# Update of the decoding states of a gated DeltaNet: full-array matmuls on masked keys, or pairs of 32-row strips on plain keys

## The chip, the cores and the metric

The kernel runs on one core of one Trainium2 chip. The metric is the time of one execution on the device in microseconds, the median of several runs. The engines are PE (TensorE, with its weight loads PEld), DVE (VectorE), ACT (ScalarE), POOL (GpSimd) and SP (SyncE, which issues most of the transfers).

## The reference

The program is one inference step of a hybrid decoder layer: a normed and modulated input of 256 prompt tokens and 8 x 4 decoding tokens goes through one large projection, three token mixers (a gated MLP over chunks, a gated DeltaNet, sparse attention) and one output projection. The change lies in the DeltaNet, in the part for the decoding tokens. For each of 16 heads and each of 8 decoding sequences there is a state S of 128 x 128 (key by value). In one chunk of 4 tokens:

```python
G = jnp.cumsum(gc, axis=-1)
...
kg = kc * jnp.exp(G[..., -1:] - G)[..., None]
gl = jnp.exp(G[..., -1])

def step(s, xs):
    qg_i, kg_i, u_i, w_i, attn_i, gl_i = xs
    v_new = u_i - jnp.einsum('bhcd,bhde->bhce', w_i, s)
    o = jnp.einsum('bhcd,bhde->bhce', qg_i, s) + jnp.einsum('bhcs,bhse->bhce', attn_i, v_new)
    s = s * gl_i[..., None, None] + jnp.einsum('bhcd,bhce->bhde', kg_i, v_new)
    return s, o
```

The last line of the step, `s = ...`, is what the changed code computes. It is an outer product over 4 tokens only, for 128 pairs of head and sequence.

## The kernel before, in words

The large projections are run as many matmuls with a moving operand of 288 columns (256 prompt and 32 decoding tokens) and weights of 128 x 128, named acc. Weights and activations are split in two parts of a shorter mantissa (wh, wl and hH, hL), so that one tile takes three matmuls: acc<-hH,wh, acc<-hL,wh and acc<-hH,wl. ACT makes wh from the loaded w (a cast), DVE makes wl (a subtraction). These matmuls form a stream that runs through the whole program.

Everything else (convolutions, DeltaNet, attention, gating) is written as small generators, called chains here, that yield where they wait for another engine. A planner, the class Weaver, runs when the program is built: it holds an estimated time for each engine and decides which chain takes its next step between two acc units. The order that results is fixed in the program; each engine runs its own list in that order. All instructions are recorded by one helper, so all rows of the profile carry its line, L71, and are told apart by the names of their tiles. Rules of the planner that matter here:

- `bank(n)` (L284) takes n of four PSUM banks for a chain and yields until they are free by the planner's estimate; `free()` gives one back.
- `calm()` (L273) holds a chain back until the planner's DMA estimate allows a transfer.
- `finish(gens)` (L245) steps the named chains, and others that can run, until they are done, without going on with the stream.
- `gmlp_open` (L2149) begins with `W.finish([DN[3]])`: the last DeltaNet group must be done before the buffers of the gating MLP are opened. It is called ahead of one fixed unit of the stream, `u[GMO].pre.append(gmlp_open)` (L2337, GMO = 12).

The DeltaNet is worked in four groups of four heads. dn_all (L1705) runs dn_group for the prompt tokens and then dn_sample (L1976) for the 32 decoding tokens of four heads, laid out as 128 rows: row 32 h + 4 b + t is head h, sequence b, token t. dn_sample loads a row of gates GB and the output gate z, clears a mask tile M, transposes q, k and v (sT), takes norms (ACT, then POOL: rr, sc), scales keys and values (kb, vb), makes kbT, the gram matrices, UA and A, and then the products with the states in blocks of 16 small matmuls on column strips (kS and qS, state_mm, L2036), between them U, Ys, vs and osm. M lies in the buffer R4, from which the prompt part of the same group writes its last output (mixD) to memory.

Then update() (L2089) is pushed as a chain of its own, beside the rest of dn_sample (the norm of the output, oTs, the write of mixD). It makes eight copies of the new values, vk[:, b], each zero outside the rows of sequence b. For the keys a tile kgm had been made, `kgm[q, hl]` = the scaled keys in the 32 rows of head hl, and zero in the other 96. For each head and each half of the sequences one matmul over all 128 rows, kgm[:, hl] by four of the vk side by side (128 x 512), gives the four outer products in one bank, named Sup; four DVE instructions (scalar_tensor_tensor) then make S * exp(g_last) + product. After a head the state is written to memory.

Of the kernel before, what the change touches and what calls it, by code (L numbers as in the profile page):

```python
# [14 lines left out]
OP = mybir.AluOpType  # L15
# [4 lines left out]
P = 128  # L20
# [67 lines left out]
class Weaver:  # L88
# [195 lines left out]
    def bank(self, n=1):  # L284

        yield
        while not self.room(n):
            yield lambda: self.room(n)
        self.take(n)
# [8 lines left out]
    def free(self, n=1):  # L298
        self.banks -= n
        self.bank_free += [self.end] * n  # L300
# [74 lines left out]
def tile_hybrid_step(ctx: ExitStack, tc: tile.TileContext, I, O):  # L375
    nc = tc.nc
    W = Weaver()
    V, A, G, T, S = (Eng(W, k, e) for k, e in zip("VAGTS", (nc.vector, nc.scalar, nc.gpsimd, nc.tensor, nc.sync)))
    dma, dma2 = S.dma_start, S.dma_start
    bank, free = W.bank, W.free  # L380
# [17 lines left out]
    def tl(pool, shape, name, bufs=1, dt=F32, tag=None):  # L398
        return W.tile(pools[pool][1], shape, dt, tag or name, name, bufs)

    def pr(name="pr"):
        t = psum.tile([P, 512], F32, tag="r", name=name, bufs=N_BANK)
        W.bank_use[t.tensor.name] = ("T", 0.0)
        return t

    def pr4(name="pr"):
        return pr(name).rearrange("p (c n) -> p c n", c=4)
# [491 lines left out]
    at_, n = [0], la_end[0] + LEAD0  # L899
# [3 lines left out]
    i = 0  # L903
    while i < len(lb):
# [4 lines left out]
        for j, u in enumerate(us):  # L909
            e = min(len(la), n0 + int(rate * (j + 1)) // PAIR * PAIR)  # L910
            W.units += [u] + la[n:e]
            n = e
        i = nxt
# [777 lines left out]
    def place(name, n):  # L1691

        t = tl("dn", [P, n * P], name, 1)

        def cut(o, *shape):
            v = t[:, o * P:(o + math.prod(shape[:-1])) * P] if len(shape) > 1 else t[:, o * P:(o + 1) * P]
            names = "abc"[:len(shape) - 1]
            if len(shape) > 1:
                v = v.rearrange(f"p ({' '.join(names)} n) -> p {' '.join(names)} n",
                                **dict(zip(names, shape[:-1])), n=shape[-1])  # L1700
            return v

        return cut

    def dn_all(g, convs):  # L1705
        yield lambda: all(c.done for c in convs) and (g - 1 in MAIN if g else X.g_smp.done)
        if g == 0:
            close_pool("ap")
            open_pool("dn")
        b = Box()  # L1710
        yield from dn_group(g, b)
        yield from dn_sample(g, b)
        if g == 3:
            close_pool("dn")
# [261 lines left out]
    def dn_sample(g, b):  # L1976
        q0 = 32 + g
        St, b_ld = b.St, b.ld
        ya, yb, ye, yf = (place(f"R{r}", 8) for r in (0, 1, 4, 5))
        GB, df, kb, vb, kbT, Pm, Y, vn0 = (ya(i, P) for i in range(8))  # L1980
        UA, AM, dec = (yb(i, 2, P) for i in (0, 2, 4))
        M = ye(0, 8, P).rearrange("p a (c n) -> p (a c n)", n=32).rearrange("p (h b n) -> p h b n", h=4, b=NB)
        kgm, vn1, os_, junk = yf(0, 4, P), yf(4, P), yf(5, P), yf(7, P)
        z = yf(6, P).rearrange("p (h t) -> p h t", h=4)
        dma2(GB, GrD[q0:q0 + 1].to_broadcast([P, P]))
        dma2(z, zD[2 + g][:, :, NPR:NTOK])
# [5 lines left out]
        pa = pr4("sT")  # L1992
# [11 lines left out]
        sc = tl("dn", [P, 6], "sc", 4)  # L2004
# [2 lines left out]
        G.tensor_tensor(sc[:, 4:5], sc[:, 0:1], eG[:, q0:q0 + 1], op=OP.mult)  # L2007
        G.tensor_scalar(sc[:, 4:5], sc[:, 4:5], -1.0, None, op0=OP.mult)
        V.tensor_scalar(df, GB, Gc[:, q0:q0 + 1], 0.0, op0=OP.subtract, op1=OP.min)
        G.memset(kgm, 0.0)  # L2010
        yield
        A.activation(kb, pa[:, 1], AF.Copy, scale=sc[:, 0:1])
        A.activation(vb, pa[:, 2], AF.Copy, scale=hbeta[:, q0:q0 + 1])
        for hl in range(4):
            q = slice(32 * hl, 32 * hl + 32)
            V.tensor_scalar(kgm[q, hl], pa[q, 1], sc[q, 2:3], None, op0=OP.mult)
        free()
        gl = tl("dn", [P, 32], "gls", 1)
        A.activation(gl, GB.rearrange("p (a t) -> p a t", t=NS)[:, :, NS - 1], AF.Exp)
# [69 lines left out]
        def update():  # L2089
            vk = place("R4", 8)(0, NB, P)  # L2090
            for b in range(NB):
                V.tensor_scalar(vk[:, b], vn1, bsel[:, b:b + 1], None, op0=OP.mult)
            for hl in range(4):
                for b0 in (0, 4):
                    yield from bank()
                    pu = pr("Sup")
                    T.matmul(pu, kgm[:, hl], vk[:, b0:b0 + 4].rearrange("p c n -> p (c n)"), start=True, stop=True)
                    yield
                    for b in range(b0, b0 + 4):
                        i = 8 * hl + b  # L2100
                        V.scalar_tensor_tensor(St[hl][:, b], St[hl][:, b], gl[:, i:i + 1],
                                               pu[:, (b - b0) * P:(b - b0 + 1) * P], op0=OP.mult, op1=OP.add)
                    free()
                yield from W.calm()
                dma(O[10][0, :, 4 * g + hl].rearrange("b d e -> d b e"), St[hl])

        MAIN[g] = True
        (up,) = W.push(update())
        yield
        r = yield from out_norm([os_], rq[:, 0:1], 1, junk)  # L2110
# [232 lines left out]
    mixed, n = [], 0  # L2343
    for i, u in enumerate(ph2):
        e = min(len(gates), int((i + 1 - GATE0) / GATE)) // GPAIR * GPAIR
        mixed += [u] + gates[n:e]
        n = max(n, e)
# [117 lines left out]
```

## Time and profile before

| | |
|---|---|
| median of 3 runs | 2639.03 us (2635.15 to 2641.7) |
| the profiled execution | 2654.27 us |
| its span, first to last instruction | 2652.5 us |
| mean granted clock of TensorE | 0.986 |
| busy: PE, PEld | 2560.9 us (97%), 2279.1 us (86%) |
| busy: DVE, ACT, POOL | 1623.5 us (61%), 1062.0 us (40%), 492.3 us (19%) |
| matmul records of Sup | 64, from 1521.7 to 2165.4 us |

The profiled execution is one run with the profiler on; its time and the durations in its rows belong together, and it is somewhat longer than the median of the timed runs. A matmul's row gives its duration from start to end; since matmuls overlap, what one costs in the stream is read from the starts of its neighbours. Consecutive records of one kind are shown as one row with their number.

### The profile page before, as it was taken

The numbers are of one execution on the slowest core, as the hardware profiler recorded it, in microseconds if no ns is written. First come the engines' busy times: TensorE is split into PE (matmuls) and PEld (weight loads), VectorE is DVE, ScalarE is ACT, GpSimd is POOL, SyncE is SP. The second block draws the span as 40 slices with busy tenths as digits, with TensorE's granted clock in tenths as the row PEclk, the third lists the DMA queues.
The fourth block names the chain that finished last, engine by engine and source line by source line (L and its number), as shares of the span: only waits on it lengthen the run. The fifth ranks groups of instructions, "written<-read, shape, count | busy, mean of one in ns | idle before, by whom it ended". The sixth has DMA issues, their size and how long they took to land.

```text
span 2652.5 us, 55324 instructions
## 1 busy us (share of the span) xinstructions
PE 2560.9 (97%) x21190; PEld 2279.1 (86%) x21190; DVE 1623.5 (61%) x3611; ACT 1062.0 (40%) x2440; POOL 492.3 (19%) x1137
## 2 busy tenths in 40 slices
PE   6999999999999999999999999999999999999997
PEld 3788888888888888877789989989989989999997
DVE  3477665555568786744467576567566567555554
ACT  3423222222245343333344444444443544444443
POOL 2000000000001042153543333343340210000000
PEclk9999999999999999999999999999999999999998
DMA  8999998998757576686776676577568565555565
GB/s 289 345 320 321 342 315 296 304 312 307 232 153 217 178 238 217 200 283 221 266 233 192 182 242 207 177 241 233 179 195 261 149 202 181 178 182 175 177 186 164
DMA packets 376032, 616.11 MB, mean 232 GB/s; under 512 B 48840, under 2 KB 149436, under 8 KB 375768
## 3 DMA queue, kind: packets, MB, share of 16 engines
q1 hardware_dynamic: 364728, 574.66, 67.8%
q0 software_dynamic: 11040, 37.92, 4.3%
q8 instruction: 167, 2.74, 0.4%
q14 instruction: 97, 0.79, 0.1%
HBM read 587.54 MB, written 24.95 MB: 231 GB/s over the span
## 4 chain that ended last, share of the span: by engine, by line
PE 86%; DMA 6%; DVE 2%; issue 2%; POOL 2%; ACT 1%; SPq 0%; another core or an unknown queue 0%; ACTq 0%; POOLq 0%; DVEq 0%
PE acc L71 68%; PE ada L71 7%; DMA wa<-in_w_ada_dram 2%; PE kT L71 1%; PE Sup L71 1%; DMA kraw<-in_cache_k_dram,ixk 1%; DVE wl L71 1%; PE YP L71 1%; DMA w<-in_w_in_dram 1%; PE v L71 1%; PE gram L71 1%; DMA vraw<-in_cache_v_dram,ixv 1%; PE o L71 1%; POOL vraw L71 1%; PE S L71 0%
## 5 line engine op out<-in xcount | busy, mean ns | idle before, releaser
L71 DVE TENSOR_TENSOR wl<-w,wh 128x512 fp32r<-128x512 f32 (+1 forms) x1216 | 806.1, 682 | 735.3 <-ACT wh L71 667.8
L71 ACT CAST wh<-w 128x512 fp32r<-128x512 f32 (+1 forms) x1216 | 717.3, 611 | 1232.3 <-PE acc L71 905.6
L71 PE MATMUL acc<-hH,wh 128*128 128x288 f32 (+1 forms) x3744 | 1180.2, 315 | 14.5 <-ACT hH L71 7.4
L71 PE MATMUL acc<-hL,wh 128*128 128x288 f32 (+1 forms) x3744 | 1110.4, 297 | 0.6 <-DVE hL L71 0.4
L71 PE MATMUL acc<-hH,wl 128*128 128x288 f32 (+1 forms) x3744 | 1108.4, 296 | 2.6 <-DVE wl L71 1.8
L71 PEld LDWEIGHTS acc<-hH,wh 128*128 128x128 f32 (+1 forms) x3744 | 708.4, 189 | 152.0 <-issue 81.9
L71 PEld LDWEIGHTS acc<-hL,wh 128*128 128x128 f32 (+1 forms) x3744 | 710.1, 190 | 6.7 <-issue 5.5
L71 PEld LDWEIGHTS acc<-hH,wl 128*128 128x128 f32 (+1 forms) x3744 | 709.1, 189 | 4.0 <-DVE wl L71 3.6
L71 PE MATMUL acc<-mL,wh 128*128 128x288 f32 x1024 | 302.6, 295 | 2.6 <-DVE mL L71 2.6
L71 PE MATMUL acc<-mH,wh 128*128 128x288 f32 x1024 | 304.4, 297 | 0.0
L71 PE MATMUL acc<-mH,wl 128*128 128x288 f32 x1024 | 302.7, 296 | 0.0
L71 PEld LDWEIGHTS acc<-mL,wh 128*128 128x128 f32 x1024 | 193.0, 189 | 2.9 <-DVE mL L71 2.9
L71 PEld LDWEIGHTS acc<-mH,wh 128*128 128x128 f32 x1024 | 193.0, 188 | 0.2
L71 PEld LDWEIGHTS acc<-mH,wl 128*128 128x128 f32 x1024 | 193.0, 188 | 0.0
L71 PE MATMUL ada<-wa,cT 128*32 128x256 f32 x2048 | 159.2, 395 | 15.8 <-DMA wa<-in_w_ada_dram 14.3
L71 PEld LDWEIGHTS ada<-wa,cT 128*32 128x32 f32 x2048 | 50.2, 109 | 66.9 <-issue 39.8
L71 DVE TENSOR_TENSOR zb<-zb,acc 128x288 f32<-128x288 f32 x160 | 70.9, 452 | 47.0 <-PE acc L71 45.7
L71 POOL TENSOR_TENSOR htmp<-yT,gaT 128x32 f32<-128x32 f32 x20 | 7.7, 382 | 460.0 <-DVE gaT L71 460.0
L71 PE MATMUL ada<-w,cT 128*32 128x256 f32 x1024 | 83.9, 393 | 1.9 <-issue 1.0
L71 POOL TENSOR_SCALAR frs<-frs 128x1 f32<-128x1 f32 (+1 forms) x3 | 0.9, 298 | 451.5 <-DVE frs L71 451.3
L71 DVE TENSOR_TENSOR R<-R,R 128x248 f32<-128x248 f32 (+30 forms) x248 | 72.6, 293 | 7.1 <-DMA R<-dD 0.5
L71 POOL TENSOR_SCALAR tap<-xp,cwT 128x32 f32<-128x32 f32 x144 | 75.8, 527 | 0.3
(457 smaller groups left out, 2387.0 us busy)
## 6 DMA issues: line engine op xcount, KB each, us to landing
w<-in_w_in_dram SPq DMA_DIRECT2D x464, 512.0 KB
wa<-in_w_ada_dram SPq DMA_DIRECT2D x160, 512.0 KB
w<-in_w_ada_dram SPq DMA_DIRECT2D x128, 512.0 KB
w<-in_w_out_dram SPq DMA_DIRECT2D x128, 512.0 KB
wa<-in_w_ada_dram SPq DMA_DIRECT2D x192, 256.0 KB
St<-in_state_dn_dram SPq DMA_DIRECT2D x16, 512.0 KB
out_dram<-St SPq DMA_DIRECT2D x16, 512.0 KB
X<-in_x_prompt_dram SPq DMA_DIRECT2D x8, 512.0 KB
```

The lines of the kernel that those rows point to most:

```text
L71: r = f(*a, **k)
```

## The change

kgm becomes kg, a tile of 128 x 128 that holds the scaled keys of all four heads, made by one DVE instruction; the memset of kgm is gone. In update() two heads are treated together: two banks are taken, and two matmuls follow each other, each on the 32 rows of its head (`tile_position=(32 * hl, 0)`), each into its own bank. Then come eight DVE instructions. The loop over the halves of the sequences lies inside the pair of heads, and the two states are written behind both halves.

```diff
--- before.py
+++ after.py
@@ -1980,7 +1980,7 @@
         GB, df, kb, vb, kbT, Pm, Y, vn0 = (ya(i, P) for i in range(8))
         UA, AM, dec = (yb(i, 2, P) for i in (0, 2, 4))
         M = ye(0, 8, P).rearrange("p a (c n) -> p (a c n)", n=32).rearrange("p (h b n) -> p h b n", h=4, b=NB)
-        kgm, vn1, os_, junk = yf(0, 4, P), yf(4, P), yf(5, P), yf(7, P)
+        kg, vn1, os_, junk = yf(0, P), yf(4, P), yf(5, P), yf(7, P)
         z = yf(6, P).rearrange("p (h t) -> p h t", h=4)
         dma2(GB, GrD[q0:q0 + 1].to_broadcast([P, P]))
         dma2(z, zD[2 + g][:, :, NPR:NTOK])
@@ -2007,13 +2007,10 @@
         G.tensor_tensor(sc[:, 4:5], sc[:, 0:1], eG[:, q0:q0 + 1], op=OP.mult)
         G.tensor_scalar(sc[:, 4:5], sc[:, 4:5], -1.0, None, op0=OP.mult)
         V.tensor_scalar(df, GB, Gc[:, q0:q0 + 1], 0.0, op0=OP.subtract, op1=OP.min)
-        G.memset(kgm, 0.0)
         yield
         A.activation(kb, pa[:, 1], AF.Copy, scale=sc[:, 0:1])
         A.activation(vb, pa[:, 2], AF.Copy, scale=hbeta[:, q0:q0 + 1])
-        for hl in range(4):
-            q = slice(32 * hl, 32 * hl + 32)
-            V.tensor_scalar(kgm[q, hl], pa[q, 1], sc[q, 2:3], None, op0=OP.mult)
+        V.tensor_scalar(kg, pa[:, 1], sc[:, 2:3], None, op0=OP.mult)
         free()
         gl = tl("dn", [P, 32], "gls", 1)
         A.activation(gl, GB.rearrange("p (a t) -> p a t", t=NS)[:, :, NS - 1], AF.Exp)
@@ -2090,19 +2087,26 @@
             vk = place("R4", 8)(0, NB, P)
             for b in range(NB):
                 V.tensor_scalar(vk[:, b], vn1, bsel[:, b:b + 1], None, op0=OP.mult)
-            for hl in range(4):
+
+            for h0 in (0, 2):
                 for b0 in (0, 4):
-                    yield from bank()
-                    pu = pr("Sup")
-                    T.matmul(pu, kgm[:, hl], vk[:, b0:b0 + 4].rearrange("p c n -> p (c n)"), start=True, stop=True)
+                    yield from bank(2)
+                    pus = []
+                    for hl in (h0, h0 + 1):
+                        pus.append(pr("Sup"))
+                        q = slice(32 * hl, 32 * hl + 32)
+                        T.matmul(pus[-1], kg[q], vk[q, b0:b0 + 4].rearrange("p c n -> p (c n)"), start=True, stop=True,
+                                 tile_position=(32 * hl, 0))
                     yield
-                    for b in range(b0, b0 + 4):
-                        i = 8 * hl + b
-                        V.scalar_tensor_tensor(St[hl][:, b], St[hl][:, b], gl[:, i:i + 1],
-                                               pu[:, (b - b0) * P:(b - b0 + 1) * P], op0=OP.mult, op1=OP.add)
-                    free()
-                yield from W.calm()
-                dma(O[10][0, :, 4 * g + hl].rearrange("b d e -> d b e"), St[hl])
+                    for hl, pu in zip((h0, h0 + 1), pus):
+                        for b in range(b0, b0 + 4):
+                            i = 8 * hl + b
+                            V.scalar_tensor_tensor(St[hl][:, b], St[hl][:, b], gl[:, i:i + 1],
+                                                   pu[:, (b - b0) * P:(b - b0 + 1) * P], op0=OP.mult, op1=OP.add)
+                        free()
+                for hl in (h0, h0 + 1):
+                    yield from W.calm()
+                    dma(O[10][0, :, 4 * g + hl].rearrange("b d e -> d b e"), St[hl])
 
         MAIN[g] = True
         (up,) = W.push(update())
```

The order that the planner makes is another. The first place is PE at the start of dn_sample for the last group: sT are the transposes of q, k and v, kbT and gram come next in that chain, and acc is the stream. Before:

```order
L71 MATMUL acc_26067<-hH_7380,wh 128x288
L71 MATMUL acc_26067<-hL_7452,wh 128x288
L71 MATMUL acc_26067<-hH_7380,wl 128x288
L71 MATMUL sT<-ident,SSG 128x128 x3
L71 MATMUL acc_26011<-hH_7380,wh 128x288
L71 MATMUL acc_26011<-hL_7452,wh 128x288
L71 MATMUL acc_26011<-hH_7380,wl 128x288
```

After:

```order
L71 MATMUL acc_26850<-hL_5268,wh 128x288
L71 MATMUL acc_26850<-hH_5196,wl 128x288
L71 MATMUL sT<-ident,SSG 128x128 x3
L71 MATMUL kbT<-ident,R_27082 128x128
L71 MATMUL gram<-R_27082,SSG 128x128
L71 MATMUL gram<-SSG 128x128
L71 MATMUL A<-ident,R_27083 128x128
L71 MATMUL kS_27142<-St_25406,R_27084 32x128
```

Before, acc matmuls follow behind sT (48 of them up to kbT). After, the whole chain follows without one.

The second place is PE at the end of the same group's update; vTk belongs to the gating MLP that is opened next. Before:

```order
L71 MATMUL Sup<-R_27182,R_26721 128x512
L71 MATMUL acc_26959<-hH_5196,wh 128x288
L71 MATMUL acc_26959<-hL_5268,wh 128x288
L71 MATMUL acc_26959<-hH_5196,wl 128x288
L71 MATMUL Sup<-R_27182,R_26721 128x512 x5
L71 MATMUL acc_26924<-hH_6288,wh 128x288
L71 MATMUL acc_26924<-hL_6360,wh 128x288
L71 MATMUL acc_26924<-hH_6288,wl 128x288
L71 MATMUL vTk<-ident,uv 128x128 x2
L71 MATMUL vTk<-ident,uv 32x128
```

After:

```order
L71 MATMUL qS_27187<-St_25409,R_27084 32x128
L71 MATMUL osm<-R_27085,R_27083 128x128
L71 MATMUL oTs<-ident,R_27085 128x128
L71 MATMUL Sup<-R_27243,R_27085 128x512 x8
L71 MATMUL acc_26801<-hH_6288,wh 128x288
L71 MATMUL acc_26801<-hL_6360,wh 128x288
L71 MATMUL acc_26801<-hH_6288,wl 128x288
L71 MATMUL vTk<-ident,uv 128x128 x2
L71 MATMUL vTk<-ident,uv 32x128
```

Before, there are acc matmuls between the first Sup, and five follow each other at the end. After, all eight stand together behind oTs, with no acc between osm and the last of them.

The third place is DVE at the same end: the row with bsel makes the eight vk, the St rows are the updates of the states, wl is the stream's subtraction, and the R row with oTs is the end of the output's norm. Before:

```order
L71 TENSOR_TENSOR R_26721<-osm,R_26721 128x128
L71 TENSOR_TENSOR wl<-w,wh 128x512
L71 TENSOR_SCALAR R_27182<-R_26721,bsel 128x128 x8
L71 TENSOR_TENSOR wl<-w,wh 128x512 x2
L71 TENSOR_SCALAR R_26721<-R_26721,onr 128x128
L71 SCALAR_TENSOR_TENSOR St_25133<-St_25133,gls,Sup 128x128 x4
L71 TENSOR_TENSOR wl<-w,wh 128x512
L71 SCALAR_TENSOR_TENSOR R_26721<-oTs,onT,R_26721 128x128
L71 SCALAR_TENSOR_TENSOR St_25133<-St_25133,gls,Sup 128x128 x4
L71 TENSOR_TENSOR wl<-w,wh 128x512
L71 SCALAR_TENSOR_TENSOR St_25134<-St_25134,gls,Sup 128x128 x8
```

After:

```order
L71 TENSOR_TENSOR R_27085<-osm,R_27085 128x128
L71 TENSOR_SCALAR R_27085<-R_27085,onr 128x128
L71 SCALAR_TENSOR_TENSOR R_27085<-oTs,onT,R_27085 128x128
L71 TENSOR_SCALAR R_27243<-R_27085,bsel 128x128 x8
L71 SCALAR_TENSOR_TENSOR St_25406<-St_25406,gls,Sup 128x128 x4
L71 SCALAR_TENSOR_TENSOR St_25407<-St_25407,gls,Sup 128x128 x4
L71 SCALAR_TENSOR_TENSOR St_25406<-St_25406,gls,Sup 128x128 x4
L71 SCALAR_TENSOR_TENSOR St_25407<-St_25407,gls,Sup 128x128 x4
```

Before, vk is made ahead of the output's scaling, with wl between. After, vk stands behind the product with oTs, and there is no wl among these rows.

## Rows read from the trace of the kernel before

**Rows 1.** The page, first and fourth part: busy time of each engine with its share of the span and its instructions; the chain that ended last by engine.

```profile
PE 2560.9 (97%) x21190; PEld 2279.1 (86%) x21190; DVE 1623.5 (61%) x3611; ACT 1062.0 (40%) x2440; POOL 492.3 (19%) x1137
...
PE 86%; DMA 6%; DVE 2%; issue 2%; POOL 2%; ACT 1%; SPq 0%; another core or an unknown queue 0%; ACTq 0%; POOLq 0%; DVEq 0%
```

**Rows 2.** Busy time by stretch, 1980 to 2140 us. Columns: length, busy time (and instructions) of PE, PEld, DVE, ACT, POOL, granted clock of TensorE, DMA share, GB/s.

```profile
1980.00:2140.00 160.00, 160.00 (x1272) 153.40 (x1275) 102.94 (x252) 78.30 (x194) 26.96 (x57) 1.00 0.65 198
```

**Rows 3.** The tile Sup, the matmuls that write it: duration of a record in ns, shortest, median, longest; first and last start; shapes. One fp32 matmul leaves two records.

```profile
L71 PE MATMUL Sup<-R,R x64: 590/592/697, 1521.7 to 2165.4; 128*128 128x512 f32 x64
```

**Rows 4.** The timeline around one Sup in the stream of acc matmuls, PE and its weight loads. Columns: start us, duration us, engine, line, operation, out<-in, tile and shape, records.

```profile
1955.36 0.29 PE L71 MATMUL acc<-hH,wl 128*128 128x288 f32 x1
...
1955.36 0.32 PEld L71 LDWEIGHTS Sup<-R,R 128*128 128x128 f32 x2
...
1955.49 1.02 PE L71 MATMUL Sup<-R,R 128*128 128x512 f32 x2
...
1956.48 0.30 PE L71 MATMUL acc<-hL,wh 128*128 128x288 f32 x1
```

**Rows 5.** The timeline of PE at two other packed matmuls in the stream: four column strips of ada, and one 32-row strip of mask (bf16).

```profile
1096.39 0.29 PE L71 MATMUL acc<-hH,wl 128*128 128x288 f32 x1
...
1096.62 0.39 PE L71 MATMUL mask<-mneg,Rm 32*128 32x512 bf16 x1
...
1097.17 0.29 PE L71 MATMUL acc<-hL,wh 128*128 128x288 f32 x1
...
2053.11 0.29 PE L71 MATMUL acc<-hH,wl 128*128 128x288 f32 x1
...
2053.33 0.64 PE L71 MATMUL ada<-w,cT 128*32 128x256 f32 x8
...
2054.14 0.29 PE L71 MATMUL acc<-hL,wh 128*128 128x288 f32 x1
```

**Rows 6.** The timeline of PE at 16 lg matmuls on a grid of 64x64 strips (two by rows, two by columns), and two acc matmuls ten steps apart.

```profile
929.67 0.30 PE L71 MATMUL acc<-hL,wh 128*128 128x288 f32 x1
...
930.99 0.29 PE L71 MATMUL acc<-hH,wl 128*128 128x288 f32 x1
...
931.22 1.10 PE L71 MATMUL lg<-kt,QI 64*64 64x128 f32 x32
```

**Rows 7.** The timeline of PE in the last group's decoding chain: the transpose ahead of it, a block of state products, the output product.

```profile
2117.44 0.38 PE L71 MATMUL oT<-ident,R 128*128 128x128 f32 x2
...
2139.84 1.08 PE L71 MATMUL kS<-St,R 128*32 128x128 f32 x32
...
2151.21 0.38 PE L71 MATMUL osm<-R,R 128*128 128x128 f32 x2
```

**Rows 8.** The timeline of POOL in the same chain; in brackets its idle time before, and what ended it.

```profile
2122.50 0.95 POOL L71 MEMSET R<- 128x1024 f32 x1 [7.52 <-DMA mixD<-R]
...
2126.26 0.20 POOL L71 TENSOR_SCALAR rr<-sq 128x2 f32<-128x2 f32 x1 [2.80 <-ACT R L71]
...
2128.44 0.23 POOL L71 TENSOR_SCALAR sc<-sc 128x1 f32<-128x1 f32 x1
...
2128.61 0.53 POOL L71 MEMSET R<- 128x512 f32 x1
...
2153.36 0.33 POOL L71 TENSOR_TENSOR onss<-onss,onr 128x1 f32<-128x1 f32 x1 [22.06 <-ACT R L71]
...
2154.94 0.21 POOL L71 TENSOR_TENSOR onr<-onr,rq 128x1 f32<-128x1 f32 x1
```

**Rows 9.** The timeline of ACT in the same chain: kb, and the square of the output.

```profile
2128.93 0.36 ACT L71 ACTIVATE R<-sT,sc 128x128 f32<-128x128 f32 x1
...
2152.82 0.31 ACT L71 ACTIVATE R<-R 128x128 f32<-128x128 f32 x1
```

**Rows 10.** The timeline of DVE in the same chain: the strip scalings of the keys, UA, the copies of q, the sum of the output, vk, and the last 24 products of the states.

```profile
2129.66 1.43 DVE L71 TENSOR_SCALAR R<-sT,sc 32x128 f32<-32x128 f32 x4
...
2136.41 0.48 DVE L71 SCALAR_TENSOR_TENSOR R<-gram,rr,R 128x256 f32<-128x256 f32 x1
...
2146.20 0.43 DVE L71 COPY R<-SSG 128x32 f32<-128x32 f32 x4
...
2151.70 0.29 DVE L71 TENSOR_TENSOR R<-osm,R 128x128 f32<-128x128 f32 x1 [2.74 <-PE osm L71]
...
2153.56 1.67 DVE L71 TENSOR_SCALAR R<-R,bsel 128x128 f32<-128x128 f32 x8
...
2162.60 6.28 DVE L71 SCALAR_TENSOR_TENSOR St<-St,gls,Sup 128x128 f32<-128x128 f32 x24
```

**Rows 11.** Busy time by stretch at two stalls and behind them, and at a shorter gap; columns as in rows 2.

```profile
1333.00:1335.60 2.60, 0.92 (x7) 0.74 (x7) 1.15 (x4) 1.69 (x5) 0.29 (x1) 1.00 0.83 329
1336.00:1339.00 3.00, 3.00 (x15) 3.00 (x15) 2.17 (x7) 0.99 (x2) 0.89 (x2) 0.50 0.15 14
2239.00:2242.00 3.00, 0.35 (x3) 0.19 (x2) 3.00 (x5) 0.89 (x2) 0.00 (x0) 1.00 0.52 156
2244.00:2250.00 6.00, 6.00 (x24) 5.65 (x25) 1.61 (x3) 1.05 (x2) 0.00 (x0) 0.50 0.25 85
1854.00:1862.00 8.00, 6.92 (x62) 6.15 (x60) 5.24 (x14) 3.00 (x10) 3.27 (x11) 1.00 0.59 167
```

**Rows 12.** The timeline of PE at the stall behind 2239 us.

```profile
2241.81 0.40 PE L71 MATMUL acc<-mL,wh 128*128 128x288 f32 x1 [2.65 <-DVE mL L71]
```


## The prediction

> **What bounds the kernel now.** I read the page's first and fourth parts first: TensorE is busy for 97% of the span and is 86% of the chain that ended last [rows 1]. Then the stretches in which the decoding states are updated: from 1980 to 2140 us PE is busy for 160.00 of 160 at the full clock, and the other engines are not [rows 2]. So an instruction taken from DVE, ACT or POOL there is worth nothing by itself, a matmul taken from PE is worth its slot in the stream, and a stretch without acc matmuls costs its whole length, since nothing later has room to catch up. Third I read the tile Sup, the target of the changed matmuls [rows 3], then single timelines for the slots, and last the order of the last group's chain, which decides.
>
> **The saving in the stream.** There are 32 Sup matmuls of 128x512 fp32 (64 records, two for each) [rows 3]; afterwards there are 16 pairs of two 32-row matmuls. In the stream acc matmuls follow each other every 0.13 us (ten steps from 929.67 to 930.99) [rows 6]. Around one Sup two acc matmuls start 1955.36 and 1956.48, two steps of 0.13 apart without it: a Sup costs 1.12 - 0.26 = 0.86 us [rows 4]. Two of them cost 1.72.
>
> A pair of row strips has no row before, so I bound it. From above: if strips take turns, 2 x 0.86 plus a switch of the tile mode. From below: if both run at once and the switch is free, 0.86. The switch: four column strips of ada (8 records of 256 columns) cost 2053.11 to 2054.14 less 0.26, so 0.77; streaming is half of what 512 columns take, 0.43, which leaves 0.34 [rows 5]. A 32-row strip of mask costs 1096.39 to 1097.17 less 0.26, so 0.52 [rows 5]; its single pass of 512 columns is half of a Sup's two, 0.21 to 0.22, and 0.30 is left. Do row strips run side by side? The 16 lg matmuls on two row and two column strips took 1.10 us in 32 records [rows 6]. A record of 128 columns is a quarter of one of 512, about 0.107, so 32 in turn would take 3.4, 16 in turn (only columns side by side) 1.7, and 8 (rows and columns side by side) 0.86 and a drain. 1.10 fits the last. I take 0.86 + 0.34 and about 0.05 for weights: 1.25 for a pair, 0.47 less than now, between 1.16 and 1.35.
>
> The Trainium skill ("TensorE: Matmul & The Clock Gate", Part 3: Packing small matmuls, row/col tiling) says that a weight load overlaps a running matmul only when the row group differs. By that rule the second pass of each strip would show its load; at the same 0.107 a pair that is about 1.7 us over 16 pairs, an estimate. The trace speaks against it: two weight loads of all 128 rows for Sup lie at 1955.36 to 1955.68, under running matmuls [rows 4]. The sum goes without it.
>
> By the order, 12 of the 16 pairs (groups 0 to 2) stand between acc matmuls: 12 x -0.47 = **-5.6 us** (-4.4 to -6.7). The four pairs of the last group are counted below.
>
> **What is removed beside it.** Four memsets of 0.53 us on POOL [rows 8], and three of the four strip scalings of each group (1.43 us for four) on DVE [rows 10]. They lie beside a full PE: 0. If that cover is gone, as in the last group below, they are worth about 0.5 us, and are left out of the chain there.
>
> **What is moved: the last group's chain.** A pair takes two of the four banks at once and the planner steps it later. In the order the last group's sT stood 48 acc matmuls ahead of its kbT, and its Sup between acc matmuls up to the last five. Now everything from sT to the eighth Sup stands behind the same acc matmul, with none between. It is run to its end by gmlp_open. ACT and DVE have no cast and no subtraction of a weight tile in it either. So PE waits through a chain that was covered. I add it up from the end of the last oT, 2117.82 in the trace [rows 7], which is now followed by 18 acc matmuls, 18 x 0.13 = 2.4 us.
> - The memset of M waits for mixD's write, which reads the same tile: 2122.50, so 4.7 after that end; it takes 0.95 [rows 8]. With 0.1 us for a hand-over (osm ends at 2151.59, DVE starts 2151.70 [rows 7, 10]) rr starts at 5.7. sT and its squares are done before that.
> - rr to sc: 2126.26 to 2128.67, 2.41 [rows 8]. Then kb on ACT, 0.26 later and 0.36 long [rows 9], so kbT starts at 8.9.
> - kbT and A are transposes as oT, of which two took 0.38 [rows 7]; with gram between, the copy on ACT at about 0.3, UA 0.48 [rows 10] and five hand-overs I put 2.0. A ends at 10.9.
> - 32 records of kS 1.08, U, 32 more: 2.6 [rows 7]; two products on DVE and the copies of q, 0.43 [rows 10], with the hand-over 0.9; qS, vs, qS again 2.6: 17.0.
> - os, osm 0.38 and the add 0.29: 0.9 [rows 7, 10]; square and its sum 0.5, POOL 2153.36 to 2155.15 1.8, hand-overs: 20.3 [rows 8, 9]. Scaling, oTs and its product: 21.5.
> - In the new order vk stands behind oTs. Four of its eight products are half of 1.67, 0.84 [rows 10]: the first pair starts at 22.4.
> - Pairs 1 and 2 take all four banks. The 24 products of St took 6.28, 0.262 each [rows 10], so a pair's eight take 2.1. Pair 3 starts when pair 1's banks are free, 25.8; pair 4 at 27.9; acc goes on at 28.9.
>
> From 2.4 to 28.9 PE has no acc: 26.5 us. The PE work in that stretch filled slots in the stream before: sT to oTs about 6.9 us with four blocks of state products at some 1.2, and eight Sup at 0.86 = 6.9, together about 13.7. The added time is 26.5 - 13.7 = **+12.8 us** (9 to 15: below, if mixD's write lands sooner or the planner's queue on SP is shorter; above, if hand-overs are 0.2 us).
>
> The Trainium skill ("TensorEngine Tiling (Array Packing)", PSUM Bottleneck) warns that packed matmuls can make emptying PSUM the limit. The rows show the same here by their own numbers: 2.1 us of DVE for a pair of about 0.9. In the stream this is hidden, here it sets pairs 3 and 4, and is in the sum.
>
> **The clock.** In this trace a stretch with little PE work is followed by the lower clock level: after 1333 to 1335.6 with 0.92 us of work, 0.50 of full clock (1.2 GHz) from 1336 to 1339; after 2239 to 2242 with 0.35, 0.50 from 2244 to 2250 [rows 11]. 1.1 us without work between 1854 and 1862 left the clock full [rows 11]. The chain begins with 6 us of nothing but sT, then is about half idle, so I expect 0.50 in most of it. The PE work on its path (four state blocks, small matmuls, three pairs) is some 7 us and would take up to 7 more; after it acc runs at half for 3 to 7 us, losing half of that, 1.7 to 3.4. Part of the chain will still be at full clock. I take **+6.5** (2 to 11).
>
> **The tail.** A wait of 2.65 us for mL at 2241.81, and the half clock behind it, are there already [rows 11, 12]. The later chain moves DVE's work and the loads ahead of it; it may go (-6) or grow (+3). I take -1.
>
> **Sum.** -5.6 + 12.8 + 6.5 - 1 = +12.7, about +13. The profiled execution took 2654.27 us, its span 2652.5 with 1.77 around it, and would become 2667; it lies 15 above the median of the runs, 2639.03, which would become **2652 us**.
>
> **Rivals.**
> - Only the idle time shows, without a fall of the clock, and the wait in the tail goes. For: the clock stayed full through the gap at 1854 [rows 11]; four blocks of kS and qS do fill PE for a while. Against: the six empty microseconds at the start. -5.6 + 12.8 - 6 = +1.2, 2640 us, chance 0.26.
> - The gain alone shows: weight tiles are fetched and cast during the stop, so the 2.65 us wait in the tail and its half clock go. It decides once the uncovered chain costs under 4 us more than its PE work, as it would if DVE, ACT and POOL, free of the stream's casts, ran it in 18 us. For: in this trace the chain's steps partly waited behind such casts. Against: the 4.7 us of mixD's write and the 4.2 us on POOL don't shrink by that. -5.6 + 4 - 6 = -8, 2631 us; chance 0.08.
> - The row strips take turns. A pair costs 1.72 + 0.34 = 2.06, 0.34 more than now instead of 0.47 less: 12 x 0.81 = +10 against the forecast, with pairs on the last chain hidden by DVE: 2661 us. Against: the 1.10 of lg [rows 6]. Chance 0.07.
> - Forecast, idle chain with a fall of the clock: 0.59.
>
> **How the numbers follow.** A measurement of this kernel can tell about 0.3%, 7.9 us, from no change. Faster by more than that is the gain alone, 0.08. Within it is the second case, 0.26. The forecast and the strips in turn are slower: 0.66. The range goes from 2638, which holds the balance case, to 2663, which holds the strips in turn and a clock at half through the chain; the forecast's own is 2645 to 2660.
>
> **What would show it.** In the profile after: Sup pairs in the stream, from the acc ahead to the second behind, 1.25 + 0.26 apart (2.3 if in turn). Between the last group's sT and its eighth Sup no acc for about 26 us or more, POOL's memset waiting for mixD, DVE's products of St as releaser of pairs 3 and 4, and PEclk at 0.50 in it or behind it. The prediction is wrong if acc matmuls run in that stretch after all, if that stretch is under 20 us, or if the stall at mL grows into a large term that I took as 1.

## The result and the profile after

The changed kernel takes 2650.88 us (median of 6 runs, 2649.76 to 2657.74) beside 2637.67 us for the kernel before on the same chip: a ratio of 1.0054, 95% interval 1.0038 to 1.0071, so 10 to 19 us slower. Forecast were 2652 us and +13.

The profiled executions stand differently to their medians: 2654.27 us before, 2649.76 us after (span 2647.8). To compare the traces all the same I count the acc matmuls, 14304 in each kernel, and take the time from number 6801, ahead of the first Sup, to the last: 1252.7 us before, 1265.4 after, 12.7 more. What differs ahead of number 6801 (17 us) lies in waits, and in the clock behind them, among instructions and an order that the change does not touch; the changed kernel profiled a second time took 9 us more up to there than the first time.

The first part of the page of after, busy time by engine as in [rows 1]:

```profile
PE 2553.9 (96%) x21190; PEld 2269.6 (86%) x21190; DVE 1621.1 (61%) x3599; ACT 1063.4 (40%) x2440; POOL 486.1 (18%) x1133
```

PE's busy time went down by 7 us and the kernel became slower. But that drop lies ahead of number 6801; from there on PE is busy 1247.0 us before and 1248.5 after, and idle 6.0 and 17.2. So some 11 of the 13 us are time in which PE stands still, and in the busy time the saving is lost again to a lower clock, as the rows below show. First the saving: a pair of Sup strips in the stream, timeline of PE, the answer to [rows 4].

```profile
1706.61 0.29 PE L71 MATMUL acc<-hH,wl 128*128 128x288 f32 x1
1706.84 1.13 PE L71 MATMUL Sup<-R,R 32*128 32x512 f32 x4
1707.90 0.40 PE L71 MATMUL acc<-hH,wh 128*128 128x288 f32 x1
1708.13 0.29 PE L71 MATMUL acc<-hL,wh 128*128 128x288 f32 x1
```

From the acc ahead to the second behind are 1.52 us; less two steps of 0.13 that is 1.26 for two heads, where two Sup cost 1.72. Then the last group's chain, timeline of PE; in brackets the idle time before a row and what ended it.

```profile
2129.92 0.38 PE L71 MATMUL oT<-ident,R 128*128 128x128 f32 x2
2132.54 0.49 PE L71 MATMUL sT<-ident,SSG 128*128 128x128 f32 x3
2137.59 0.48 PE L71 MATMUL kbT<-ident,R 128*128 128x128 f32 x1 [4.57 <-ACT R L71]
2138.42 0.79 PE L71 MATMUL gram<-R,SSG 128*128 128x128 f32 x2 [0.35 <-ACT R L71]
2140.29 0.47 PE L71 MATMUL A<-ident,R 128*128 128x128 f32 x1 [0.65 <-DVE R L71]
2140.69 1.94 PE L71 MATMUL kS<-St,R 128*32 128x128 f32 x32
2146.66 1.08 PE L71 MATMUL qS<-St,R 128*32 128x128 f32 x32
2150.91 0.47 PE L71 MATMUL oTs<-ident,R 128*128 128x128 f32 x1 [2.75 <-DVE R L71]
2152.61 8.52 PE L71 MATMUL Sup<-R,R 32*128 32x512 f32 x16 [1.23 <-DVE R L71]
...
2161.06 0.61 PE L71 MATMUL acc<-hH,wh 128*128 128x288 f32 x1
```

No acc runs from 2132.54 to 2161.06: 28.5 us. The gaps before kbT, oTs and the first Sup are the chain's own waits. What they wait for stands on POOL and DVE (timelines of the same stretch, the answers to [rows 8, 10]):

```profile
2134.97 0.95 POOL L71 MEMSET R<- 128x1024 f32 x1 [7.50 <-DMA mixD<-R]
2135.89 0.19 POOL L71 TENSOR_SCALAR rr<-sq 128x2 f32<-128x2 f32 x1
```

```profile
2151.69 1.65 DVE L71 TENSOR_SCALAR R<-R,bsel 128x128 f32<-128x128 f32 x8
2154.72 8.36 DVE L71 SCALAR_TENSOR_TENSOR St<-St,gls,Sup 128x128 f32<-128x128 f32 x32 [1.38 <-PE Sup L71]
```

The memset waited for mixD's write until 2134.97, 4.67 after the last oT ended; the 32 products of St ran without a break, 0.26 each, and the strips of the last two pairs waited for their banks one by one. That is seen from their weight loads, 1.03 us apart, the time of four products (timeline of PEld):

```profile
2155.96 0.50 PEld L71 LDWEIGHTS Sup<-R,R 32*128 32x128 f32 x2 [1.14 <-issue]
...
2159.06 0.50 PEld L71 LDWEIGHTS Sup<-R,R 32*128 32x128 f32 x2 [0.54 <-PE Sup L71]
```

Busy time and granted clock by stretch, columns as in [rows 2]:

```profile
2133.00:2138.00 5.00, 0.43 (x2) 0.18 (x1) 1.44 (x7) 1.69 (x9) 2.52 (x7) 0.86 0.72 222
2138.00:2142.00 4.00, 3.00 (x34) 2.32 (x37) 1.01 (x3) 0.64 (x3) 1.14 (x3) 0.50 0.02 4
2142.00:2146.00 4.00, 3.85 (x79) 2.84 (x72) 0.98 (x6) 0.27 (x1) 0.00 (x0) 0.82 0.00 0
2146.00:2150.00 4.00, 2.16 (x45) 1.45 (x37) 0.29 (x1) 1.04 (x4) 0.69 (x3) 1.00 0.01 4
2150.00:2153.00 3.00, 0.86 (x3) 0.57 (x5) 1.86 (x9) 0.00 (x0) 0.46 (x2) 0.55 0.00 0
2153.00:2161.00 8.00, 8.00 (x16) 2.78 (x14) 6.62 (x27) 0.00 (x0) 0.00 (x0) 0.50 0.31 83
2161.00:2164.00 3.00, 3.00 (x14) 2.78 (x14) 2.16 (x10) 0.52 (x2) 0.00 (x0) 0.51 0.82 245
2164.00:2168.00 4.00, 4.00 (x35) 3.93 (x35) 0.69 (x1) 2.92 (x11) 0.00 (x0) 1.00 0.98 250
```

The clock fell to 0.50 behind the empty 5 us, came back within the chain, fell again behind the 2.75 us for oTs, and stayed down for all Sup and 3 us of the stream.

The new order loses time at a second place too, ahead of this one, in the prompt part of the third group. There the first two kbT stand behind acc number 8712; in the old order, with the same Sup pairs (e10_change_in_old_order below), they stand behind 8754. ACT, which makes their input, has itself been held up by a transfer (timelines of PE and ACT, busy time by stretch):

```profile
1743.10 0.33 PE L71 MATMUL kbT<-ident,R 128*128 128x128 f32 x1 [2.04 <-ACT R L71]
```

```profile
1740.61 0.20 ACT L71 ACTIVATE gl<-R 128x2 f32<-128x2 f32 x1 [2.64 <-DMA R<-GrD]
```

```profile
1744.00:1747.00 3.00, 3.00 (x16) 3.00 (x15) 1.23 (x3) 0.49 (x3) 2.71 (x7) 0.52 0.58 175
```

PE waits 2.04 us, and the clock is at half behind it. From acc 8698 to 8863 the changed kernel takes 34.5 us, the change in the old order, which has no such wait there, 30.3.

### The profile page after: what moved, and what is told of

Its sections match the earlier page's. It is cut to its first block, busy times and chain, and to the rows that moved or that the text cites. A ratio compares the mean times of both kernels' runs of the same rounds, so it can differ in the third digit from the quotient of the medians.

```text
span 2647.8 us, 55303 instructions
## 1 busy us (share of the span) xinstructions
PE 2553.9 (96%) x21190; PEld 2269.6 (86%) x21190; DVE 1621.1 (61%) x3599; ACT 1063.4 (40%) x2440; POOL 486.1 (18%) x1133
## 5 line engine op out<-in xcount | busy, mean ns | idle before, releaser
L71 PE MATMUL acc<-hH,wh 128*128 128x288 f32 (+1 forms) x3744 | 1168.2, 312 | 12.6 <-ACT hH L71 7.3
L71 PE MATMUL ada<-wa,cT 128*32 128x256 f32 x2048 | 160.1, 394 | 14.0 <-DMA wa<-in_w_ada_dram 12.8
```

What stands on the lines that cost most here:

```text
L71: r = f(*a, **k)
```

## The experiments

Theory F is the forecast: strips save 0.47 us for a pair, and the loss is the last group's chain, which the planner's new order leaves uncovered. The rival R1: taking two banks at once, or the changed instructions themselves, cost the time in all groups. Ratios are to runs of before on the same chip, with 95% intervals; those medians of before moved from 2638 to 2647 us between the chips. In the diffs, `...` marks what is left out of a line.

**Pairs without strips, and strips in the same order** (e1_masked_pairs, e2_strips_same_order). The first has the change's loop on the masked copies:

```diff
-                        T.matmul(pus[-1], kg[q], vk[q, b0:b0 + 4]..., tile_position=(32 * hl, 0))
+                        T.matmul(pus[-1], kgm[:, hl], vk[:, b0:b0 + 4]...)
```

> The kernel before, with the loop of the change (two heads and two banks at a time) but still with the masked copies and two full-array matmuls of 128 rows. In its order the last group's chain stays among acc matmuls up to the first pair of Sup; only the last six Sup stand together. Theory F (the loss is the uncovered chain of the last group; strips save 0.47 us for a pair): nothing is saved, six Sup in a row go at the pace of DVE's products, 6.3 us in place of 5.2, so 0 to +3 us against before, 2637 to 2641. Rival R1 (the loss comes from taking two banks at once, which shifts the order of all groups): +8 us or more, 2646 and up.

Measured: 2641.57 us, ratio 1.0006 (0.9992 to 1.002). Taking two banks and two heads at a time costs nothing that can be told from 0. The second differs in the matmul alone, `kgm[q, hl]` by `vk[q, ...]` with its tile position; the planner charges it the same, so every engine's order is the same.

> As e1_masked_pairs, with the same order of instructions, but each Sup is a matmul on the 32-row strip of its head (read from the masked copies, which are still made), two heads side by side. Theory F: 13 pairs in the stream at 0.47 us less each, the last three pairs at DVE's pace, so 5 to 7 us under e1_masked_pairs, 2631 to 2635. Rival R1: the strips are not what decides, within 2 us of e1_masked_pairs. Rival R2 (strips take turns): 5 us or more above it.

Measured: 2632.61 us, ratio 0.9969 (0.9957 to 0.998), 9 us under the first by medians, with intervals that leave room for 5 to 7. By the count from acc 6801 its trace is only 1.3 us shorter than that of the first; but it holds a wait of 1.27 us for a transfer (prev) and a stretch at a lower clock behind it, 3.3 us together, that the first has not. So a single trace doesn't settle the size; two more traces with strips in this order follow below. The signs are settled: R2 falls, the strips gain, and the pairs of banks don't lose 8 us, against R1.

**The stop alone** (e3_stop_before). Before, with one call more:

```diff
+        if not n:
+            u[24].pre.append(lambda: W.finish([DN[3]]))
```

> The kernel before, unchanged but for one more call that runs the last group's chain to its end 18 acc matmuls behind the last oT, so that sT to the eighth Sup stand without acc between, as in the changed kernel. No strips, one bank at a time. Theory F: the stop costs what it costs in the changed kernel beside its saving, 13 + 6 = 19 us, with 8 single Sup 1 us more: +16 to +21 us against before, 2654 to 2659. Rival R1: the stop is only a part, +3 to +10, 2641 to 2648.

Measured: 2656.15 us beside 2638.67, ratio 1.0055 (1.0036 to 1.0073), so 10 to 19 us; by the acc count +13.4. Its chain, timeline of PE:

```profile
2104.52 0.38 PE L71 MATMUL oT<-ident,R 128*128 128x128 f32 x2
2107.13 0.49 PE L71 MATMUL sT<-ident,SSG 128*128 128x128 f32 x3
2112.13 0.48 PE L71 MATMUL kbT<-ident,R 128*128 128x128 f32 x1 [4.50 <-ACT R L71]
2126.64 0.33 PE L71 MATMUL oTs<-ident,R 128*128 128x128 f32 x1 [2.75 <-DVE R L71]
2128.29 8.79 PE L71 MATMUL Sup<-R,R 128*128 128x512 f32 x16 [1.32 <-DVE R L71]
...
2136.51 0.69 PE L71 MATMUL acc<-hH,wh 128*128 128x288 f32 x1
```

These are the waits of the changed kernel, 4.50 for 4.57 and 2.75 for 2.75, and 29.4 us without acc, in a kernel that has no strips. The stop by itself makes before as slow as the change. The clock came back to full under its eight whole Sup, and the stream behind ran at 1.00:

```profile
2128.00:2132.00 4.00, 3.71 (x5) 1.70 (x6) 2.08 (x10) 0.00 (x0) 0.00 (x0) 0.57 0.11 16
2132.00:2136.00 4.00, 4.00 (x10) 1.71 (x9) 4.00 (x16) 0.00 (x0) 0.00 (x0) 1.00 0.48 135
2136.00:2140.00 4.00, 4.00 (x27) 3.46 (x26) 3.90 (x14) 0.62 (x1) 0.00 (x0) 1.00 0.89 261
```

By the ratio (+14.5) and the count the stop cost less than the 16 to 21 expected; the stream at full clock behind it is one part of that, and the whole stop had been priced too high, as the part on the prediction shows.

**The changed kernel with another estimate** (e4_told_planner). One factor in the planner's cost:

```diff
-            n = _size(ins[1])
+            n = _size(ins[1]) * (0.72 if ins[0].shape[0] == 32 and ins[0].shape[-1] > 32 else 1.0)
```

> The changed kernel, with one estimate of the planner changed: a matmul on 32 rows is charged 0.72 of the full one, near half a pair's measured 1.25 us. The instructions are the same; in the new order the last group's chain lies among acc matmuls up to osm, and only oTs and the four pairs of Sup (16 records) stand together at the end. Theory F: 12 pairs save 5.6 us; the last four go at DVE's pace, some 8 us without acc in place of 6.9 us of Sup in the stream, with a short wait ahead of them: -2 to -5 us against before, 2633 to 2636. Rival R1: the loss stays, 2645 and up.

Measured: 2642.34 us, ratio 1.0008 (0.9997 to 1.002). It regains most of the loss (by the ratio 2 of 14 us are left), but not the expected 2633 to 2636. The step of this expectation that failed is "a short wait" ahead of the last pairs. In its timeline of PE:

```profile
2144.61 0.33 PE L71 MATMUL oTs<-ident,R 128*128 128x128 f32 x1 [3.19 <-DVE R L71]
2144.86 7.79 PE L71 MATMUL Sup<-R,R 32*128 32x512 f32 x16
2152.59 0.61 PE L71 MATMUL acc<-hH,wh 128*128 128x288 f32 x1
```

The wait was 3.19, the clock fell behind it (0.56 from 2145 to 2150), and from the last acc (2141.12) to the next are 11.5 us, where some 8 were expected. Also the order changed from acc 6228 on, far ahead of the first Sup, so this is no clean comparison.

**Strips without a partner** (e5_strip_alone). The loop of before, one head and one bank at a time:

```diff
-                    T.matmul(pu, kgm[:, hl], vk[:, b0:b0 + 4]...)
+                    T.matmul(pu, kg[q], vk[q, b0:b0 + 4]..., tile_position=(32 * hl, 0))
```

> The changed kernel's keys (no masked copies, matmuls on the 32-row strip of a head), but in the loop of before: one head, one bank and one Sup at a time, so that no strip has a partner. In its order the last group's chain lies among acc matmuls. Theory F (the gain comes from two strips side by side, a strip alone pays the switch of the tile mode): a Sup costs 0.86 + 0.30 to 0.34 in place of 0.86, about 28 of them between acc matmuls, so +8 to +10 us against before, 2646 to 2649. Rival R3 (a matmul on 32 rows is cheaper by itself): not above before, 2638 or less.

Measured: 2655.81 us beside 2646.06, ratio 1.0035 (1.0022 to 1.0049), 6 to 13 us slower; +9.5 by the acc count. Timeline of PE:

```profile
1722.87 0.29 PE L71 MATMUL acc<-hH,wl 128*128 128x288 f32 x1
1723.09 1.12 PE L71 MATMUL Sup<-R,R 32*128 32x512 f32 x2
1724.14 0.40 PE L71 MATMUL acc<-hH,wh 128*128 128x288 f32 x1
1724.38 0.30 PE L71 MATMUL acc<-hL,wh 128*128 128x288 f32 x1
```

1.51 less 0.26 is 1.25 us, the same as a pair: the second strip is free, and one alone costs 0.39 more than the masked matmul, against R3.

**The opening moved** (e6_strips_later_open, e7_before_later_open, e8_after_open28, e9_before_open28). First with the strips of the second experiment, and with before:

```diff
-GMO = 12
+GMO = 14
```

> As e2_strips_same_order, with the opening of the gating MLP (the call that forces the last group's chain to its end) two units of the stream later (14 in place of 12). In its order all 16 pairs of Sup stand among acc matmuls, none is forced. Theory F (a pair of strips side by side costs 1.25 us in place of 1.72, and the changed kernel loses only by the forced chain): 16 x -0.47 = -7.5 us against e7_before_later_open, so 2629 to 2633. If the strips gave nothing, within 2 us of e7.

> Control: the kernel before with the same call two units later. Five of its eight last Sup still stand together. Theory F: nothing on the path changes, within 2 us of before, 2637 to 2641.

Measured: 2639.59 us, ratio 0.9992 (0.9978 to 1.0006), and 2644.31 us, 1.0014 (1.0003 to 1.0026). The later opening costs before some 4 us, a little more than expected; the strips lie 4.7 us under it by medians, 6.3 by the acc count (16 pairs, 7.5 expected). The 2629 to 2633 us put for them were missed; on this chip before itself took 2641.08.

Then with the changed kernel, and with before:

```diff
-GMO = 12
+GMO = 28
```

> The changed kernel with the opening of the gating MLP 16 units later (28 in place of 12). In its order the last group's chain is back among acc matmuls up to the second pair; the last two pairs stand together. The later opening may cost something at the start of the output projection, as much as in e9_before_open28. Theory F: the stop was the whole loss, so 5 to 7 us under e9_before_open28. Rival R1 (the loss lies in the order of the groups, from taking two banks): 5 us or more above it.

> Control for e8_after_open28: the kernel before with the same opening at unit 28. Its last chain lies among acc matmuls as it did. Theory F: before plus what the late opening costs, which the rows before do not show: 0 to +15 us.

Measured: 2651.01 us, ratio 1.0044 (1.0027 to 1.0061), and 2650.86 us, 1.0034 (1.0021 to 1.0047). A miss: the changed kernel is not under its control, they are equal within their intervals. Its chain is covered, and another stop has come, in the timeline of PE:

```profile
2190.70 0.61 PE L71 MATMUL acc<-mH,wh 128*128 128x288 f32 x1 [8.91 <-ACT mH L71]
```

The output projection waits for its first input, since the gating MLP was opened late. Of the control there is no trace that can be set beside it. A part of the missing gain can be placed all the same: the changed kernel with the late opening has the wait at the third group's kbT too (2.02 us), some 4 us with the clock behind it, and the control, whose order is that of before up to the last group, should not have it, since the trace of before has none there. That leaves 1 to 3 of the expected 5 to 7 us, which the intervals allow but do not show.

**The change in the old order** (e10_change_in_old_order, with e11_strips_again and e12_changed_again beside it). The clean undo: every instruction of the change is kept, and the planner alone is told of what is gone.

```diff
+        W.note("G", "memset", (kgm, 0.0), {})
...
         V.tensor_scalar(kg, pa[:, 1], sc[:, 2:3], None, op0=OP.mult)
+        for hl in range(1, 4):
+            W.note("V", "tensor_scalar", (kgm[:, hl], pa[:, 1], sc[:, 2:3]), {})
```

> The changed kernel with all its instructions (no masked copies, no memset of them, pairs of strips), but the planner is told of the memset and the three strip scalings that are gone, as if they were still issued. It then makes the order of e2_strips_same_order, in which the last group's chain lies among acc matmuls up to its first pair. Theory F: the time of e2_strips_same_order within 2 us, 5 to 9 us under before, and 14 to 20 us under the changed kernel run beside it; the removed memsets and scalings themselves are worth nothing. Rival R1 (something in the changed instructions costs the time, not their order): 8 us or more over e2.

> e2_strips_same_order once more, beside the other two on one chip. Theory F: 5 to 9 us under before.

> The changed kernel once more, beside the other two on one chip: 11 to 16 us above before.

Measured on one chip beside 2646.71 us of before: 2639.34 us, ratio 0.9976 (0.9966 to 0.9987); 2640.15 us, 0.9977 (0.9963 to 0.9991); 2659.98 us, 1.0049 (1.003 to 1.0068). The same instructions in two orders lie 20.6 us apart (14 to 20 expected), one faster than before by 3 to 9 us, the other slower by 8 to 18. Keeping or dropping memsets and scalings makes 0.8 us between the first two medians: nothing that can be told from 0. R1 falls for good: two banks at once and the changed instructions are in the fast kernel too. By the traces the two orders differ in two places. From acc 10153 to 11008, around the last group, the changed kernel takes 171.0 us (171.5 in its second profile), the change in the old order 156.0: 15.0 to 15.5. From 8698 to 8863, at the third group's kbT, it takes 34.5 (both) against 30.3: some 4. So Theory F names the larger loss and not the whole of it. In the first one's timeline of PE, the end of the last group:

```profile
2149.02 1.37 PE L71 MATMUL Sup<-R,R 32*128 32x512 f32 x8
2151.53 2.12 PE L71 MATMUL Sup<-R,R 32*128 32x512 f32 x4 [1.15 <-DVE St L71]
2153.59 0.59 PE L71 MATMUL acc<-hH,wh 128*128 128x288 f32 x1
```

From the first of these Sup to the next acc are 4.6 us, where sT to acc were 28.5 in the changed kernel: the order is not free of the effect, only most of it is gone. This version, and the second experiment, which is as fast, beat both kernels.

The lengths from acc 6801 to the last, against before, in one table:

```
                                   us against 1252.7
changed kernel, two profiles       +12.7  +13.7
the stop alone in before           +13.4
strips without a partner            +9.5
pairs of masked matmuls             -3.4
strips in that order, twice         -4.7   -5.4
the change in the old order         -6.9
```

2.0 of the -3.4 and 2.0 of the -4.7 lie behind acc 11201, past the last Sup, where the others show 0.1 to 0.9: masked pairs are some -1.4 up to there.

## Why the prediction was right

- **The price of a pair**: 1.25 forecast, 1.26 by the rows of after. 12 pairs at 0.46 are 5.5. From acc 6801 to 10601, where the 12 pairs of the first three groups lie in the old order, masked pairs measure -1.4 against before, strips -6.8 (the change in the old order), -6.1 and -4.0 (the second experiment, twice; the -4.0 holds the 3.3 us at the wait for prev). So strips gain 5.4 and 4.7 on masked pairs, and 2.6 with that wait in it. -5.6 stands, to about 1 us. One of the 12 gained nothing: its records took 1.66 in place of 1.13 (1513.57 us), the strips one behind the other.
- **The parts of that price** were right in sum; what they consist of stays open. I had set the Trainium skill's rule aside ("TensorE: Matmul & The Clock Gate", Part 3: Packing small matmuls, row/col tiling: a weight load overlaps a running matmul only when the row group differs), because loads of whole Sup lie under matmuls [rows 4]. The trace of a strip alone does not agree with the rule either: the load of its second pass stands under its first pass, which runs on the same rows from 1723.09 to 1723.78. All the same the passes lie further apart. Two records of a strip alone span 1.12 and the shorter is 0.59 long, so the second starts 0.53 behind the first; for a whole Sup it is 1.02 less 0.59, 0.43. These 0.10 are as long as the 0.107 put for an exposed load, but no row shows a load in them, and their cause stays open. The rest of the 0.39 lies ahead of the first pass, behind the last and at the second acc.

```profile
1716.39 1.02 PE L71 MATMUL Sup<-R,R 128*128 128x512 f32 x2
```

```profile
1723.20 0.18 PEld L71 LDWEIGHTS Sup<-R,R 32*128 32x128 f32 x1
```

(A whole Sup, in the timeline of PE of the pairs without strips; the second load of a strip alone, in the timeline of PEld of the strips without a partner.)

- **What lies beside PE is worth nothing**: shown, as far as 0.8 us can be told from 0, by the change with and without the copies.
- **The chain is uncovered**: 26.5 us without acc forecast at full clock, 28.5 measured, with the half clock inside it. The first pair of Sup was forecast 22.4 after the last oT and started 22.3 after it (2152.61 less 2130.30). POOL's steps from rr to sc were shorter (2135.89 to 2137.74, 1.85 for 2.41), matmuls at half clock longer (kS 1.94 for 1.08), so that this near hit is partly luck. The 2 us lie behind it: from the first Sup to the next acc are 8.45 for 6.5, since the last four strips ran one by one where pairs were forecast, and at half clock.
- **The clock**: +6.5 forecast. Its fall was there, but not for the whole chain, and the stream ran at half for 3 us behind, 1.5 lost. 28.5 less the 13.7 that the work cost before, and 1.5, make 16.3, against 12.8 + 6.5 = 19.3 forecast for both: this pair of terms was 3 too high as rows show it. The comparison of the two orders gives 15.0 to 15.5 for the last group, so 4 too high.
- **The tail**: -1 forecast for the wait for mL; it stayed, 2.15 in place of 2.65 [rows 12], -0.5 by the count (434.3 before, 433.8 after, from acc 11201 to the last).

```profile
2235.44 0.47 PE L71 MATMUL acc<-mL,wh 128*128 128x288 f32 x1 [2.15 <-DVE mL L71]
```

- **The sum**: the mechanism is the one forecast, but that +13 was met so closely is luck. The chain and its clock were put some 4 us too high, and some 4 us were lost at the third group's kbT, a wait that the prediction does not have: it looked for what the new order uncovers in the last group alone.

Of the rivals, "only the idle time shows" fell by the clock's rows, "the gain alone" by the 28.5 us, the strips in turn by the pair's 1.26.

## What to carry to other kernels

Where a planner lays out a program, the change that is written is not the change that runs: read the new order for stretches in which the bounding engine has one chain and nothing else, and add those up before the saving. Look also for steps that moved ahead of what they wait for: in a full stream one wait of 2 us cost 4 here, with the clock behind it. Telling the planner of instructions that are no longer issued separates the two, and here turned a loss of 13 us into a gain of 6. Packing two row strips pays when both are there at the same moment; one alone is slower than the full-array matmul with zeros (1.25 us for 0.86 here).

## What was not expected

- A strip's cost does not depend on its partners: one took 1.25 us in the stream, two 1.26. Four strips of two pairs ran side by side as well: 8 records in 1.37 us (2149.02 above; three started together and the fourth 0.28 behind), where two pairs in the stream take 2.26 of records.
- The granted clock came back from 0.50 in the middle of the chain, with PE busy 3.85 of 4 us with small matmuls of state products (2142 to 2146). The same chain with whole Sup was back at 1.00 from 2132 to 2136, that with strips stayed at 0.50 through 8 us in which PE's records fill the time as well. No run here shows why.
